# Second block: positions' tables are made in the first block; projections, outputs and feed-forward begin and end with one token tile ahead of the other

## The chip, the cores and the metric

The kernel runs on one core of a Trainium2 chip. The metric is the device time of one execution in microseconds (us); lower is better. Three executions of the kernel before took 2748.75, 2737.08 and 2747.66 us, median 2747.66.

Engines are named as the profile names them: PE (TensorE, matmuls), PEld (its weight loads), DVE (VectorE), ACT (ScalarE), POOL (GpSimd), SP (SyncE, which here issues every DMA).

## The reference, cut to what matters

Two transformer blocks of two layers each run one after the other over 256 tokens of width 1024, in float32. The change lies in the second block:

```python
def second_block(x, positions, ...):
    cos, sin = rope_tables(positions)
    for l in range(DEPTH):                                   # 2
        h = rms_norm(x, attn_pre_norm[l])
        mix = hybrid_mixer(h, cos, sin, w_in[l], ...)        # h @ w_in, three attentions, @ w_out
        x = x + rms_norm(mix, attn_post_norm[l])
        h = rms_norm(x, ffn_pre_norm[l])
        x = x + rms_norm(conv_ffn(h, w_up[l], conv_w[l], conv_b[l], w_down[l]), ffn_post_norm[l])
    return x

def rope_tables(positions):
    inv_freq = ROPE_THETA_2 ** (-2.0 * jnp.arange(half, dtype=jnp.float32) / ROPE_DIM)
    ang = positions.astype(jnp.float32)[..., None] * inv_freq
    return jnp.cos(ang)[:, :, None, :], jnp.sin(ang)[:, :, None, :]

def conv_ffn(h, w_up, conv_w, conv_b, w_down):               # w_up: 1024 x 5632, w_down: 2816 x 1024
    u = h @ w_up
    ...                                                      # causal convolution of 3 taps along the tokens
    a, b = jnp.split(c, 2, axis=-1)
    return (jax.nn.silu(a) * b) @ w_down
```

Each `rms_norm` needs a whole row of 1024, so a matmul that follows one can begin for a token only when the matmul before the norm has ended for that token in all of its columns.

## The kernel before, in words

The 256 tokens lie in two **token tiles** of 128 (tile 0 and tile 1). All large products are made from pairs: every float32 operand is split into a rounded `hi` part and the remainder `lo`, and `mm3` (L220 to L222) issues three matmuls for each pair of 128 x 128 weights. Weights come by DMA as `raw` blocks of 128 x 1024 (512 KB); ACT makes `hi` (L210, a cast) and DVE makes `lo` (L213, a subtraction) before PE can use them. The blocks of raw lie in a ring of a few buffers: SP issues the next one when the DVE subtraction has emptied a buffer.

`gemm_t` takes the activations as the stationary operand, so one matmul serves one token tile and 512 columns of output. It runs through blocks of weights (4 rows of 128 each) and does tile 0, then tile 1, for every block; the last `tail` blocks are held back and done for tile 0 first and then for tile 1. `gemm_f` (the up projections of the feed-forward) takes the weights as the stationary operand, so each of its matmuls covers 256 columns, the tokens of both tiles.

A layer of the second block is: `rms_hT` (norm, transposes, split), `attend` with six projections `proj(0)` to `proj(5)` (512 columns each, the last one 284) and the attention, `wide` (output projection, 2 column halves of 512, 8 rows of weights), `add_rms`, `rms_hT`, 22 up projections of 256 columns with the convolution between (L475, L477), `down` (2 column halves, 22 rows of weights), `add_rms`.

Between two products stands this chain for each tile, which I call a **seam**: L411 (ACT, squares of one column half), L412 (DVE), L274 and L275 (POOL, inverse root), L419 (DVE, adds into the stream X), L369 (ACT, squares of X), L274 and L275 again, L376 (ACT, tile 0) or L374 (DVE, tile 1) for the scaled row, 8 transposes on PE (L385 where `apart` is set: a PSUM tile holds 4 of them, all of one token tile; L395 otherwise: a PSUM tile holds both token tiles), and the split of the transposed tile: L313 (ACT) and L314 (DVE), in pieces of 128 or 256 columns. There are four seams that matter here: A, from the first block into layer 1; B, from `wide` into the feed-forward of layer 1; C, from `down` of layer 1 into layer 2; D, as B, in layer 2. At A the chain begins in the first block's own norm (L1012 to L1044).

The order of the instructions on each engine is not written out by hand: the framework's scheduler simulates the program and sets one queue per engine, and every engine takes its queue in that order. A matmul that stands behind a transpose in PE's queue waits when the transpose waits.

`positions` makes the sine and cosine tables of the second block: 11 small DVE operations on tiles of 128 x 16 and two ACT operations that need another function table (L346, L347). `consts2` casts two constant matrices. Both are called at the begin of the second block.

## Time and profile before

| what | value |
|---|---|
| three runs | 2748.75, 2737.08, 2747.66 us; median 2747.66 |
| the profiled execution | 2742.06 us, of which 2740.2 us is the span from its first to its last instruction |
| PE busy | 2640.3 us (96%) |
| DVE, ACT, POOL busy | 1955.6 us (71%), 1383.8 us (50%), 136.0 us (5%) |
| mean granted TensorE clock | 0.98 |
| first block, second block | about 0 to 2014 us, 2014 to 2740 us |

All terms in the text are differences against the profiled execution; the time to be predicted is a median of runs, which stands 5.6 us (0.2%) above that execution.

### The profile page before, as it was taken

What the parts mean: (1) busy time and instruction counts of PE and PEld (TensorE: products, weight loads), DVE (VectorE), ACT (ScalarE), POOL (GpSimd) and SP (SyncE); (2) the same over time, 40 slices, a digit from 0 to 9 for tenths busy, and PEclk for the clock granted to TensorE, in tenths of its full rate; (3) what the DMA queues carried; (4) which work ended last, traced back from release to release, by engine and by line L of the source; (5) the groups of instructions that cost most, each with busy time, mean ns of one, the idle gap of its engine ahead of it and who ended that gap; (6) DMA issues with size and microseconds to landing.
All of it is one profiled execution on the core that took longest, in us unless ns stands there. A gap on an engine that the chain in (4) does not pass through costs nothing.

```text
span 2740.2 us, 44882 instructions
## 1 busy us (share of the span) xinstructions
PE 2640.3 (96%) x17024; PEld 2260.7 (83%) x17024; DVE 1955.6 (71%) x3942; ACT 1383.8 (50%) x2524; POOL 136.0 (5%) x280
## 2 busy tenths in 40 slices
PE   7999999999999999999999999989999999999999
PEld 5877999977889888887797898879976699776897
DVE  4988977888866633345688997666666698556895
ACT  3555565545545422234745654544454566544663
POOL 0010011000001100002100100010010000000000
PEclk9999999999999999999999999989999999998999
DMA  7566556565535522222555433545554256542454
GB/s 255 185 229 205 170 171 217 173 205 177 178 116 193 185 85 93 93 96 91 155 170 202 156 128 116 169 154 193 186 186 156 89 185 195 173 149 80 167 192 155
DMA packets 127912, 443.29 MB, mean 162 GB/s; under 512 B 14888, under 2 KB 19112, under 8 KB 127696
## 3 DMA queue, kind: packets, MB, share of 16 engines
q1 hardware_dynamic: 127696, 440.43, 48.7%
q8 instruction: 134, 2.20, 0.3%
q14 instruction: 82, 0.67, 0.1%
HBM read 435.09 MB, written 5.28 MB: 161 GB/s over the span
## 4 chain that ended last, share of the span: by engine, by line
PE 87%; DVE 4%; DMA 3%; ACT 3%; issue 1%; POOL 1%; SPq 0%; DVEq 0%; POOLq 0%; ACTq 0%
PE g L221 20%; PE g L220 20%; PE g L222 20%; PE t L221 3%; PE t L222 3%; PE t L220 3%; DMA raw<-in_w_dram 2%; PE g L919 2%; PE t L1142 2%; PE t L1168 1%; PE t L1270 1%; PE t L1255 1%; PE t L1105 1%; DVE lo L213 1%; PE g L663 1%
## 5 line engine op out<-in xcount | busy, mean ns | idle before, releaser
L213 DVE TENSOR_TENSOR lo<-raw,hi 128x512 fp32r<-128x512 f32 (+2 forms) x1280 | 825.3, 684 | 350.4 <-issue 156.7
L210 ACT CAST hi<-raw 128x1024 fp32r<-128x1024 f32 (+2 forms) x644 | 671.9, 1045 | 723.9 <-PE g L221 252.3
L220 PE MATMUL g<-b,hi 128*128 128x256 f32 (+1 forms) x2912 | 831.1, 287 | 2.5 <-ACT hi L210 1.8
L221 PE MATMUL g<-b,hi 128*128 128x256 f32 (+1 forms) x2912 | 827.7, 286 | 2.7 <-DVE b L311 2.6
L222 PE MATMUL g<-b,lo 128*128 128x256 f32 (+1 forms) x2912 | 822.3, 287 | 1.6 <-DVE lo L213 1.6
L220 PEld LDWEIGHTS g<-b,hi 128*128 128x128 f32 x2912 | 548.2, 189 | 13.5 <-ACT b L310 2.4
L221 PEld LDWEIGHTS g<-b,hi 128*128 128x128 f32 x2912 | 548.6, 188 | 12.4 <-DVE b L311 4.3
L222 PEld LDWEIGHTS g<-b,lo 128*128 128x128 f32 x2912 | 541.5, 188 | 11.0 <-DVE lo L213 2.7
L1282 DVE SCALAR_TENSOR_TENSOR yc<-yc,vec,yc 128x256 f32<-128x256 f32 x720 | 345.7, 480 | 10.9
L221 PE MATMUL g<-lo,b 128*128 128x512 f32 (+2 forms) x712 | 271.8, 382 | 1.8 <-DVE lo L213 1.7
L220 PE MATMUL g<-hi,b 128*128 128x512 f32 (+2 forms) x712 | 253.5, 376 | 11.8 <-ACT hi L210 6.2
L222 PE MATMUL g<-hi,b 128*128 128x512 f32 (+2 forms) x712 | 264.2, 371 | 0.5 <-DVE b L314 0.4
L220 PEld LDWEIGHTS g<-hi,b 128*128 128x128 f32 x712 | 134.0, 191 | 38.6 <-ACT hi L210 7.0
L221 PEld LDWEIGHTS g<-lo,b 128*128 128x128 f32 x712 | 135.7, 191 | 30.5 <-DVE lo L213 6.3
L222 PEld LDWEIGHTS g<-hi,b 128*128 128x128 f32 x712 | 135.3, 190 | 22.2 <-DVE b L314 1.1
L220 PE MATMUL t<-b,hi 128*128 128x256 f32 (+1 forms) x336 | 111.9, 333 | 0.0
L221 PE MATMUL t<-b,hi 128*128 128x256 f32 (+1 forms) x336 | 111.9, 333 | 0.0
L222 PE MATMUL t<-b,lo 128*128 128x256 f32 (+1 forms) x336 | 111.7, 332 | 0.0
L919 PE MATMUL g<-raw,cs 128*32 128x512 f32 x384 | 84.4, 637 | 12.4 <-DMA raw<-in_w_dram 12.2
L477 DVE SCALAR_TENSOR_TENSOR s<-g,vec,s 128x255 f32<-128x255 f32 (+1 forms) x176 | 84.2, 478 | 6.0 <-ACT s L475 3.8
L221 PEld LDWEIGHTS t<-b,hi 128*128 128x128 f32 x336 | 63.2, 188 | 7.5
L220 PEld LDWEIGHTS t<-b,hi 128*128 128x128 f32 x336 | 63.1, 188 | 7.4
(421 smaller groups left out, 3924.1 us busy)
## 6 DMA issues: line engine op xcount, KB each, us to landing
raw<-in_w_dram SPq DMA_DIRECT2D x772, 512.0 KB
b<-in_row_dram SPq DMA_DIRECT2D x16, 512.0 KB
b<-in_ctx_dram SPq DMA_DIRECT2D x4, 512.0 KB
ends<-st SPq DMA_DIRECT2D x8, 256.0 KB
st<-ends SPq DMA_DIRECT2D x8, 256.0 KB
b<-in_x_dram SPq DMA_DIRECT2D x4, 512.0 KB
b<-ctx SPq DMA_DIRECT2D x4, 512.0 KB
raw<-in_w_dram SPq DMA_DIRECT2D x4, 426.0 KB
```

Source lines behind the costliest of these rows:

```text
L210: self.nc.scalar.copy(hi[:, :m], p)
L213: self.nc.vector.tensor_sub(lo[:, q], p[:, q], hi[:, q].bitcast(F32))
L220: t.matmul(ps, a[0], b[0], start=first, stop=False)
L221: t.matmul(ps, a[0], b[1], start=False, stop=False)
L222: t.matmul(ps, a[1], b[0], start=False, stop=last)
L477: nc.vector.scalar_tensor_tensor(c[:, m, j:], ps[:, m, :256 - j], cw[:, ft, 2 - j:3 - j], c[:, m, j:], op0=ALU.mult, op1=ALU.add)
L663: nc.tensor.matmul(ps[:, b], qk['nq', a * per + b][s, t * 128:t * 128 + 128], qk[kn, 0][s, :nk], start=False, stop=b == per - 1)
L919: nc.tensor.matmul(ps[32 * q:32 * q + 32], self.cs[:, h * 4 + q], raw[:, q % 2 * 512:q % 2 * 512 + 512], start=h == 0, stop=h == 1, tile_p ...
L1105: nc.tensor.matmul(p[:, h], kw[:, d, h * 128:h * 128 + 128], vg[:, h * 256:h * 256 + 256], start=True, stop=True)
L1142: nc.tensor.matmul(o, w, self.U[d][:, b * 256:b * 256 + n], start=d + i == 0, stop=d + i == 2)
L1168: nc.tensor.matmul(ps[:, a, h], G[h][b][:, a] if b < 3 else kT[:, h, ts], G[h][b][:, 2 + a], start=True, stop=True)
L1282: e.scalar_tensor_tensor(o, y[:, j:j + 256], w[:, j:j + 1], o, op0=ALU.mult, op1=ALU.add)
```

## The change

- `consts2` and `positions` are called in the first block, ahead of its last feed-forward, and their tiles go to the pool that lives through the whole program. `positions` loads the 128 x 8 table of frequencies by a DMA of its own.
- `attend` calls `proj(1, 2)` first, then `proj(5)`; `proj(1)` used to come later, behind the gates. With `ahead=2` both of its blocks are the tail, so tile 0 goes through all 8 rows of weights before tile 1. All its weights lie in the buffers of tag `zh` (those of the feed-forward's z tiles).
- `wide` calls the steps of its two column halves in turn, one at a time; it called one step of each half and then two of each.
- In the feed-forward `rms_hT` is called with `apart` set, and the first two up projections (f = 0) are made with the activations stationary, tile by tile: 48 matmuls of 256 columns for each tile, an ACT copy of 128 x 512 out of PSUM and 4 transposes back for each tile.
- `down` holds back 1 block in its first half and 3 in its second (1 and 2 before).
- A scratch area of the DMAs is set to 1024 bytes.

```diff
-                hi = self.tile(pool or self.slot(), [128, cols], F32R, tag or 'hi')
-                lo = self.tile(pool or self.W, [128, cols], F32R, tag or 'lo')
+                th, tl = tag if isinstance(tag, tuple) else (tag or 'hi', tag or 'lo')
+                hi = self.tile(pool or self.slot(), [128, cols], F32R, th)
+                lo = self.tile(pool or self.W, [128, cols], F32R, tl)
...
-    def positions(self, pos):
-        nc = self.nc
+    def positions(self, pos, freq):
+        nc = self.nc
+        fq = self.tile(self.S, [128, 8], F32, 'freq')
+        nc.sync.dma_start(fq, freq)
...
-        self.identb = self.tile(self.P, [128, 128], BF16, 'identb')
+        self.identb = self.tile(self.C, [128, 128], BF16, 'identb')
...
-        def proj(c):
+        def proj(c, ahead=0):
+
             n = 512 if c < 5 else 284
             pss = [self.tile(self.PG, [128, 512], F32, 'g')[:, :n] for _ in range(2)]
-            self.gemm_t(pss, xs, self.blocks(lambda h: src('in', c, h) if c < 5 else src('inr', 0, h), 8, n))
+            tiles = self.blocks(lambda h: src('in', c, h) if c < 5 else src('inr', 0, h), 8, n, ahead, (self.P, 'zh', 512))
+            self.gemm_t(pss, xs, tiles, tail=ahead or 1)
...
-            for n in (1, 2):
+            for _ in range(3):
                 for st in steps:
-                    for _ in range(n):
-                        next(st, None)
+                    next(st, None)
             return pss
         self.add_rms(X, wide, row[:, :D])
 
 
-        hT = self.rms_hT(X, v[:, V2['fn']:V2['fn'] + 8])
+        hT = self.rms_hT(X, v[:, V2['fn']:V2['fn'] + 8], True)
         cw = v[:, V2['cw']:].rearrange("p (f j) -> p f j", j=4)
         zh, zl = [], []
+
+        ws = [self.weights(src('up', e), 8, 256, *at) for e, at in enumerate(((), (self.P, 'zh', 512)))]
+        first = []
+        for t in range(2):
+            ts = slice(t * 128, t * 128 + 128)
+            ps = self.tile(self.PG, [128, 512], F32, 'g')
+            for e, w in enumerate(ws):
+                for k in range(8):
+                    self.mm3(ps[:, e * 256:e * 256 + 256], (hT[0][:, k, ts], hT[1][:, k, ts]), w[k], e + k == 0, e == 1 and k == 7)
+            y = self.tile(self.P, [128, 512], F32, 's2')
+            nc.scalar.copy(y, ps)
+            first = first or [self.tile(self.PT, [128, 2, 256], F32, 't') for _ in range(2)]
+            for e in range(2):
+                for m in range(2):
+                    col = e * 256 + m * 128
+                    nc.tensor.transpose(first[e][:, m, ts], y[:, col:col + 128], self.ident)
         for f in range(11):
             cc = []
             for half in range(2):
-                w = self.weights(src('up', 2 * f + half), 8, 256)
-                ps = self.tile(self.PG, [128, 2, 256], F32, 'g')
-                self.gemm_f([ps[:, m] for m in range(2)], w, lambda k: (hT[0][:, k], hT[1][:, k]))
+                if f == 0:
+                    ps = first[half]
+                else:
+                    w = self.weights(src('up', 2 * f + half), 8, 256)
+                    ps = self.tile(self.PG, [128, 2, 256], F32, 'g')
+                    self.gemm_f([ps[:, m] for m in range(2)], w, lambda k: (hT[0][:, k], hT[1][:, k]))
...
-            self.gemm_t(ps, zs, self.blocks(lambda h: src('down', c, h), 22, 512, 2 * c, (self.P, 'zh', 512)), tail=1 + c)
+            self.gemm_t(ps, zs, self.blocks(lambda h: src('down', c, h), 22, 512, 2 * c, (self.P, 'zh', 512)), tail=1 + 2 * c)
...
         nc = self.nc
+        proj(1, 2)
         proj(5)
...
         nc.vector.scalar_tensor_tensor(lf, z, 0.0, e, op0=ALU.min, op1=ALU.subtract)
-        proj(1)
...
                     else:
+                        K.consts2(I['cm'])
+                        n, m = AT2['freq']
+                        K.positions(I['pos'], I['cst2'][:, n:n + m])
                         K.pend = left(K.ffn(L, X))
```

Since the scheduler sets the queues, the program's own order is shown at three places. In the rows of the changed kernel, line numbers lie 1 to 3 higher: L211 is the cast L210, L221 to L223 are the three matmuls L220 to L222, L372, L379, L388 and L414 are L369, L376, L385 and L411.

**ACT at seam C**, from the first tile's last squares to the second tile's norm. Names: `ms_...77` and `ms_...94` belong to tile 0's sums, `b_1720` and `b_1721` are tiles 0 and 1 of X, `h<-raw` are weights of `proj(1)`, `hi<-raw` of 852 and 284 columns are weights of `proj(5)`. Before:

```order
L411 ACTIVATE b_4079_24086,ms_4077_24084<-g_24305 128x512
L369 ACTIVATE b_4158_24531,s_n_4162_24538<-b_1720_10158 128x1024
L411 ACTIVATE b_4080_24087,ms_4078_24085<-g_24306 128x512
L376 ACTIVATE b_4158_24531<-b_1720_10158,s_n_4164_24541 128x512 x2
L313 ACTIVATE b_4170_24559<-t_24560,vec_3468_20826 128x128
L313 ACTIVATE b_4170_24559<-t_24573,vec_3468_20826 128x128
L369 ACTIVATE b_4159_24532,s_n_4167_24551<-b_1721_10159 128x1024
```

The same place after the change:

```order
L414 ACTIVATE b_4096_24136,ms_4094_24134<-g_24355 128x512
L211 CAST h_4199_24672<-raw_24666 128x512
...
L372 ACTIVATE b_4175_24581,s_n_4179_24588<-b_1720_10158 128x1024
L211 CAST h_4209_24692<-raw_24686 128x512
L414 ACTIVATE b_4097_24137,ms_4095_24135<-g_24356 128x512
L211 CAST hi_24760<-raw_24758 128x852
L211 CAST h_4212_24698<-raw_24696 128x512
L379 ACTIVATE b_4175_24581<-b_1720_10158,s_n_4181_24591 128x512 x2
L211 CAST hi_24767<-raw_24765 128x284
L211 CAST h_4214_24702<-raw_24696 128x512
L372 ACTIVATE b_4176_24582,s_n_4184_24601<-b_1721_10159 128x1024
```

Where no cast stood, nine now stand inside the chain: seven of 128 x 512 (three of them in the line of "..."), one of 852 and one of 284 columns.

**PE at seam C**, changed kernel, from tile 0's transposes on (`b_4175` is tile 0, `b_4176` tile 1):

```order
L388 MATMUL t_24610<-cst_6_81,b_4175_24581 128x128 x4
L388 MATMUL t_24623<-cst_6_81,b_4175_24581 128x128 x4
L221 MATMUL g_24664<-h_4197_24668,b_4187_24609 128x512
L222 MATMUL g_24664<-h_4198_24669,b_4187_24609 128x512
L388 MATMUL t_24636<-cst_6_81,b_4176_24582 128x128 x4
L388 MATMUL t_24649<-cst_6_81,b_4176_24582 128x128 x4
L223 MATMUL g_24664<-h_4197_24668,b_4187_24609 128x512
```

Two matmuls of tile 0 stand between the two tiles' transposes; before, 8 matmuls of 284 columns stood there. At seam A these are 6 of 512 columns, and 6 of 284 before.

**PE at seam B**, changed kernel, the same place (`b_3859` is tile 0, `b_3860` tile 1):

```order
L388 MATMUL t_22432<-cst_6_81,b_3859_22403 128x128 x4
L388 MATMUL t_22445<-cst_6_81,b_3859_22403 128x128 x4
L221 MATMUL g_22518<-hi_22486,b_3871_22431 128x256
L222 MATMUL g_22518<-lo_22487,b_3871_22431 128x256
L223 MATMUL g_22518<-hi_22486,b_3871_22431 128x256
...
L388 MATMUL t_22458<-cst_6_81,b_3860_22404 128x128 x4
L388 MATMUL t_22471<-cst_6_81,b_3860_22404 128x128 x4
L223 MATMUL g_22518<-hi_22486,b_3871_22431 128x256
```

Eight matmuls of tile 0 (three shown) stand between the tiles' transposes, where none stood before; the other 88 of the first two up projections come behind tile 1's transposes. D is the same. Ahead of B, the last matmuls of `wide` stand as before: both kernels end it with 10 matmuls of tile 1 for one column half and 10 for the other. The last matmuls of `down` are 20 of tile 0 and then 20 of tile 1; they were 18 and 18.

## Rows read from the trace of the kernel before

**Rows 1.** The page: busy time and share of PE; the chain that ended last, by engine.

```profile
PE 2640.3 (96%) x17024; PEld 2260.7 (83%) x17024; DVE 1955.6 (71%) x3942; ACT 1383.8 (50%) x2524; POOL 136.0 (5%) x280
...
PE 87%; DVE 4%; DMA 3%; ACT 3%; issue 1%; POOL 1%; SPq 0%; DVEq 0%; POOLq 0%; ACTq 0%
```

**Rows 2.** Waits of PE, 2014 to 2740 us: total us, times, longest.

```profile
PE t L385 <- ACT b L376: 7.7, 2, 5.7
PE t L395 <- DVE b L374: 6.1, 2, 3.2
...
PE t L395 <- ACT b L376: 3.3, 2, 1.9
```

**Rows 3.** Seam A, timeline: start us, us, engine, line, operation [idle <-releaser].

```profile
2019.78 1.97 PE L385 MATMUL t<-cst,b 128*128 128x128 f32 x8 [5.69 <-ACT b L376]
2024.75 1.11 PE L385 MATMUL t<-cst,b 128*128 128x128 f32 x4
...
2024.61 1.28 ACT L347 ACT_TABLE_LOAD   x1
2025.91 0.22 ACT L347 ACTIVATE cs<-ang 128x16 f32<-128x16 f32 x1
...
2044.76 1.28 ACT L444 COPY proj<-g 128x512 f32<-128x512 f32 x2 [1.76 <-PE g L222]
...
2024.21 0.48 DVE L374 TENSOR_SCALAR b<-b,s_n 128x512 f32<-128x512 f32 x1
```

**Rows 4.** What a piece of work takes: casts, subtractions, splits, arrival of a raw block.

```profile
2163.67 3.73 ACT L210 CAST h<-raw 128x512 fp32r<-128x512 f32 x7
...
2164.32 4.30 DVE L213 TENSOR_TENSOR h<-raw,h 128x512 fp32r<-128x512 f32 x7 [0.55 <-ACT h L210]
...
2026.41 1.92 DVE L314 SCALAR_TENSOR_TENSOR b<-t,vec,b 128x128 fp32r<-128x128 f32 x6 [0.44 <-ACT b L313]
...
2356.24 3.50 SPq L190 DMA_DIRECT2D raw<-in_w_dram  x4
...
2360.13 1.14 ACT L210 CAST h<-raw 128x512 fp32r<-128x512 f32 x2 [2.75 <-DMA raw<-in_w_dram]
```

**Rows 5.** Seam C, timeline.

```profile
2366.58 0.39 PE L220 MATMUL g<-h,h 128*128 128x512 f32 x1
...
2370.43 0.39 PE L222 MATMUL g<-h,h 128*128 128x512 f32 x1
2372.80 1.27 PE L385 MATMUL t<-cst,b 128*128 128x128 f32 x8 [1.98 <-ACT b L376]
...
2377.24 1.91 PE L385 MATMUL t<-cst,b 128*128 128x128 f32 x8
...
2372.02 1.33 ACT L376 ACTIVATE b<-b,s_n 128x512 f32<-128x512 f32 x2 [0.42 <-POOL s_n L275]
...
2396.78 1.28 ACT L444 COPY proj<-g 128x512 f32<-128x512 f32 x2 [1.73 <-PE g L222]
...
2376.50 0.88 DVE L374 TENSOR_SCALAR b<-b,s_n 128x512 f32<-128x512 f32 x2
```

**Rows 6.** Seam B, timeline: the transposes of tile 1.

```profile
2185.80 1.97 PE L395 MATMUL t<-cst,b 128*128 128x128 f32 x8 [3.16 <-DVE b L374]
```

**Rows 7.** Windows: length; busy (instructions) of PE, PEld, DVE, ACT, POOL; granted clock; DMA share; GB/s.

```profile
2186.00:2192.00 6.00, 6.00 (x30) 5.94 (x30) 3.43 (x9) 3.15 (x8) 0.00 (x0) 0.54 0.01 3
2192.00:2200.00 8.00, 8.00 (x73) 8.00 (x72) 5.48 (x10) 4.09 (x5) 0.00 (x0) 1.00 0.42 131
2376.00:2380.00 4.00, 4.00 (x20) 3.94 (x21) 3.24 (x11) 2.36 (x9) 0.47 (x1) 0.59 0.00 0
2549.00:2555.00 6.00, 5.63 (x32) 5.57 (x33) 4.01 (x10) 3.15 (x8) 0.00 (x0) 0.64 0.01 3
...
0.00:40.00 40.00, 25.75 (x108) 8.12 (x108) 8.13 (x23) 8.70 (x14) 3.04 (x26) 0.91 0.87 290
40.00:2014.00 1974.00, 1927.85 (x12566) 1674.92 (x12565) 1431.18 (x2801) 984.93 (x1784) 116.64 (x219) 0.99 0.49 161
```

More of the change, by code (lines that the diff above doesn't have):

```diff
@@ L263, in blocks @@
             hs[-2:] = hs[:-3:-1]
-        own = hs[len(hs) - last:]
-        return [(4 * h, lambda h=h: self.weights(src(h), min(4, n - 4 * h), ncol, *(at if h in own else ()))) for h in hs]
+        own = dict(zip(hs[len(hs) - last:], at if at and isinstance(at[0], tuple) else (at,) * last))
+        return [(4 * h, lambda h=h: self.weights(src(h), min(4, n - 4 * h), ncol, *own.get(h, ()))) for h in hs]
     def small(self, fam, n=8):
@@ L356, in consts2 @@
         for t in range(2):
-            b = self.tile(self.P, [128, 512], BF16, f'cmb{t}')
+            b = self.tile(self.C, [128, 512], BF16, f'cmb{t}')
             nc.vector.tensor_copy(b, raw[:, t * 512:t * 512 + 512])
@@ L1763, in build @@
             K.c = lambda n: c2[:, AT2[n][0]:AT2[n][0] + AT2[n][1]]
-            K.consts2(I['cm'])
-            K.positions(I['pos'])
             for l in range(2):
```

4 lines of the change are left out of this document (2 added, 2 removed).

## The prediction, made before the changed kernel was run

> **What bounds the kernel now.** The page comes first: PE is busy for 2640.3 of 2740.2 us, and the chain that ended last runs through PE for 87% of the span [rows 1]. DVE (71%) and ACT (50%) matter only where PE waits for them. The changed kernel issues the same matmuls and 16 more transposes, so time can only come from PE's waits and from stretches at the lower clock. The next view is therefore the waits of PE in the second block. Three kinds belong to the seams: 7.7 us for L376 with tile-wise transposes (A 5.7, so C 2.0), 6.1 us for L374 (B 3.2, D 2.9), 3.3 us for L376 at B and D [rows 2]. That is 17.1 us, about 0.6% of the run, and most of it is a chain that the change keeps. The timeline of each seam tells what the wait is for, and the windows tell the clock: behind the waits it is granted 0.54 at B and 0.64 at D, near the lower of the two levels (1.2 and 2.4 GHz), and 1.00 right behind that [rows 7].
>
> **The change part by part.** What matters is when tile 1's transposes can start, since nearly all of PE's work stands behind them, and PE's queue keeps its order. I call that moment the restart.
>
> *`wide`:* the diff lets tile 0 end earlier, but the program's order shows the same last 20 matmuls of tile 1 in both kernels. The scheduler had already done it. Term: 0.
>
> *`down`:* tile 0 ends 20 instead of 18 matmuls ahead. A matmul of 512 columns takes 0.2265 us ((2370.43 − 2366.58) / 17 [rows 5]), so tile 0's chain starts 0.45 us earlier; this is inside the walk of seam C. At the program's end tile 1's chain is last in both kernels: 0.
>
> *Seam C.* PE ends at 2370.66 (the last matmul's start [rows 5] and one step); I count from there. Before, L376 starts at +1.36, L374 at +5.84, the restart is at +6.58 [rows 5]. Now nine weight casts and their subtractions stand inside this chain. A cast of 128x512 takes 0.53 us (3.73 / 7), a subtraction 0.61 us (4.30 / 7) [rows 4]; the 852-column cast I scale to 0.9 us. Walking both queues with these: tile 0's L369 starts at −0.95, since a subtraction stands ahead of L419; tile 1's L411 starts at +0.8 behind one cast; two casts (0.9 and 0.55) hold L376 until +2.95; tile 1's L369 starts at +5.15, L374 at +7.35, restart at about +8.1. So the restart is 1.5 us later. Ahead of it PE does 2 matmuls of 512 columns (0.45 us) where it did 8 of 284 (each 284/512 of 0.2265, 0.126; 1.0 us): another 0.55 us. Against that, from 2377.24 to the copy at 2396.78 [rows 5] PE took 19.5 us for 17.9 us of work at full clock (1.27 for transposes, 40 × 0.126, 48 × 0.2265, 0.7 for six small matmuls): 1.6 us went to waits and the lower clock, and a restart with more splits ready may save some. Between +0.45 (all of the 1.6 saved) and +2.05 (none) I take **+1.5**. Bounds: −1 if the casts find idle time and the restart does not move; +5 if all nine (3.73 + 0.9 + 0.3) lie in series.
>
> *Seam A.* The same with eight casts and subtractions of `proj(1)` and two of `proj(5)` in the norm's chain. `positions` leaves: 1.28 us of table load, 2 × 0.22 us on ACT [rows 3], about 2.7 us of small DVE work, and a reload of the gates' table. In the walk tile 0's L376 is 0.9 us later, tile 1's L1042 1.1 us later (behind three subtractions), its L369 2.3 us later (behind five casts), and L374 moves from 2024.21 [rows 3] to about 2027.5: 3.3 us. What `positions` gave back is in that; most of it stood behind the point where the chain is now held. Restart at 2028.0; behind it lie 1.27 + 42 × 0.2265 + 48 × 0.126 = 16.8 us. Before, 2024.75 to 2044.76 [rows 3] took 20.0 us for 18.1 us of work, of which 0.7 us (the small matmuls) now comes later and is not counted. With the same loss of 1.9 us the end is at 2046.7 against 2044.1: +2.6; with no loss +0.7. One more wait: the second 852-column block can be issued only when a subtraction at about 2026.8 has emptied its buffer, and a block arrives 3.9 us after its issue (2356.24 to 2360.13 [rows 4]). ACT stands at its cast then, ahead of the split of row 2: up to +0.9. I take **+2.5**; bounds −2.5 (restart unmoved, no loss) and +4.
>
> The Trainium skill, ScalarE: Activation LUTs, section What ACT_TABLE_LOAD costs, gives a table load about 1.28 us and a drain of about 1.38 us beside it. The trace has the 1.28 us, and the next operation 0.02 us behind it [rows 3], so no drain is seen. By the page A would get up to 1.4 us more back.
>
> *Where `positions` goes:* the scheduler puts it at the program's start, some 25 us in. There the DMA is the pace (0.87 busy, PE 25.75 of 40 us [rows 7]), which hides it: 0. Without that cover it costs about 5 us (two table loads of 1.28, 0.44 for the tables, about 2 for the small operations). The matrices' casts fall into the first block's feed-forward, 0.
>
> *Seams B and D.* PE now has eight matmuls of tile 0 ahead of tile 1's transposes, but tile 1's chain, which set the restart at 2185.80 [rows 6], is as long as before, and a few splits stand in it: 0.15 us later. Of the wait of 3.16 us [rows 6] only 8 × 0.11 us (8.00 / 73 [rows 7]) = 0.9 us is filled with work; the rest of the wait remains. The transposes back are 8 more, 1.27 us at full clock [rows 5]. That is +0.5 us at each. The splits are 16 pieces of 128 columns, each 0.32 us on DVE (1.92 / 6 [rows 4]), 5.1 us together, less than the 40 matmuls of tile 0 and the transposes need meanwhile: hidden; if not, 1 us. The clock pays: at B 30 matmuls and transposes took 6.0 us where 0.11 each would be 3.3, so 2.7 us lost; at D 5.63 against 3.5, 2.1 us lost [rows 7]. At C, where a few matmuls lie between the two tiles' transposes, the clock was back (0.59 in 2376 to 2380) within about 3 us of the first of them, sooner than at B. I take half as regained: B 0.5 − 1.3 = **−0.8**, D 0.5 − 1.0 = **−0.5**. Bounds: −2.2 and −1.6 (all regained), +1 each (none, and a split late).
>
> Sum: 1.5 + 2.5 − 0.8 − 0.5 = **+2.7 us**. On the profiled execution (2742.06) that is 2744.8, on the median (2747.66) 2750.4. The three runs spread over 11.7 us, so I do not trust either to the us, and predict the middle, **2748 us**.
>
> **The rivals.**
>
> 1. *The clock is not regained.* The few matmuls between the transposes are too thin, and the stretch behind the restart is as slow as now. For it: at B the matmuls run near the lower level although 8 transposes had run right ahead of them [rows 6, 7]. Against it: C. B and D are then +0.5 each, the sum +5.0: about 2750.
> The Trainium skill, TensorE: Matmul & The Clock Gate, section Part 4: PE-mode transpose, says that transposes do not count as PE activity the way matmuls do. By that rule the transposes that now come earlier would earn no clock, which is this case; the trace does not separate it from the plain effect of the wait.
>
> 2. *It hides what it is built to hide.* The casts find idle slots of ACT and DVE (C −1, A −2.5) and the clock comes back at once (B −2.2, D −1.6): −7.3 us, some 2738. For it: ACT is half idle [rows 1]. Against it: in the seam ACT is the chain.
>
> 3. *The casts lie in the chain one after the other, and a block of weights comes late* (the other side). Place: ACT's queue at C, where the 852-column cast stands ahead of tile 0's L376. It decides once that block arrives later than about +1.6 us, which is when my walk has it arrive, 3.9 us behind a subtraction that ends at −2.25: then L376, both tiles and PE wait for a DMA. Price: up to the +5 of C and +4 of A, with +1 for B and D: +10 us, some 2756.
>
> 4. *The scheduler's new order of the first block matters.* About 7% of PE's rows there stand elsewhere. PE is idle for 46 of 1974 us in it [rows 7]; were a third of that added or taken away, which is my guess of how far an order can go, it would be 15 us either way.
>
> **How the numbers follow.** Forecast 0.50 (its own range 2742 to 2754), rival 1 0.17, rival 2 0.13, rival 3 0.12, rival 4 0.08, half on each side. A measurement of this kernel can tell about 0.5%, 13.7 us, from no change: below 2734 or above 2761. Forecast and rival 1 lie inside. Rival 2 gets past 2734 one time in four, rival 4's good half most times: 0.06. Rival 3 gets past 2761 one time in three, rival 4's bad half most times: 0.08. The range leaves out half of rival 4 on each side and the tails of rivals 2 and 3: 2736 to 2760.
>
> **What would show it.** In the profile after: at C L376 some 1.6 us and tile 1's transposes some 1.5 us later against the end of `down`, with casts of `h` between L411 and L376; at A tile 1's transposes about 3 us later against the first block's last matmul, and no table load ahead of the splits; at B and D a wait of 1 to 2 us ahead of tile 1's transposes with eight matmuls ahead of it, and fewer slow matmuls behind. I am wrong where tile 1's transposes come earlier at A or C, where ACT waits for a raw block ahead of L376, or where the first block's length differs by more than 5 us.

## The result, and the profile after

| kernel | median of the runs | profiled execution | span | PE busy |
|---|---|---|---|---|
| before | 2747.4 us (4 runs, 2737.1 to 2748.8) | 2742.06 us | 2740.2 us | 2640.3 us |
| after | 2783.3 us (4 runs, 2780.5 to 2786.4) | 2781.47 us | 2779.6 us | 2670.7 us |

The ratio is 1.0134, 95% interval 1.0115 to 1.0154: slower by about 37 us. The prediction was 2748 us with a range up to 2760, so it was wrong. Line numbers of after are 1 higher than before up to L314 (L313 before), 3 higher up to L422, 23 higher behind the feed-forward.

The page of after, against [rows 1]:

```profile
PE 2670.7 (96%) x17040; PEld 2289.2 (82%) x17040; DVE 1954.8 (70%) x3958; ACT 1391.8 (50%) x2556; POOL 136.6 (5%) x280
...
PE 22%; ACT 1%; DVE 1%; DMA 1%; issue 0%; POOL 0%; DVEq 0%; POOLq 0%; ACTq 0%; SPq 0%
```

The first line already says that the prediction looked in the wrong place. Of the 39 us between the spans PE is idle for 9 and busy for 30, with 16 instructions more, and 16 transposes are worth 2.5 us at the 1.27 us that 8 of them take at full clock [rows 5]. (The second line is of no use: the chain could be followed back for a quarter of the span only.) The waits of PE from seam A on, against [rows 2], account for little of it:

```profile
PE t L388 <- ACT b L379: 17.3, 4, 6.4
PE g L221 <- ACT b L314: 7.4, 4, 3.3
...
PE g L221 <- ACT hi L211: 1.3, 2, 1.1
```

The 17.1 us of the three seam waits before are 17.3 us now, all ahead of tile 0's transposes (L388, which stands where L385 and L395 stood), and new are 7.4 us in which the early matmuls of tile 0 wait for its splits (L314). So busy PE has to be read next, and since the granted clock is 1.00 nearly everywhere, by how many matmuls it gets done. Windows of PE over 25 us of the feed-forward in layer 1 and in layer 2; first before, then after (length, busy, number of matmuls, clock, DMA share, GB/s):

```profile
2220.00:2245.00 25.00, 25.00 (x223) 1.00 0.60 197
2583.00:2608.00 25.00, 25.00 (x223) 1.00 0.59 194
```

```profile
2254.00:2279.00 25.00, 25.00 (x214) 1.00 0.56 190
2616.00:2641.00 25.00, 25.00 (x214) 1.00 0.56 187
```

PE is never idle in these windows, the clock is the full one in all four, the work is the same (256 columns, `gemm_f`), and after does 4% fewer matmuls. The timeline shows the step, before:

```profile
2250.17 0.28 PE L221 MATMUL g<-b,hi 128*128 128x256 f32 x1
2250.28 0.28 PE L222 MATMUL g<-b,lo 128*128 128x256 f32 x1
2250.40 0.28 PE L220 MATMUL g<-b,hi 128*128 128x256 f32 x1
```

and after:

```profile
2250.23 0.28 PE L223 MATMUL g<-b,lo 128*128 128x256 f32 x1
2250.35 0.28 PE L221 MATMUL g<-b,hi 128*128 128x256 f32 x1
2250.47 0.28 PE L222 MATMUL g<-b,hi 128*128 128x256 f32 x1
```

The duration of one (0.28) is the same; the distance from start to start is 0.113 before and 0.118 to 0.12 after. I took it from the starts of all neighbouring matmuls of equal width at full clock: with 256 columns 115.08 ns before (9250 pairs) and 118.44 after (9273); with 512 columns 231.9 and 232.8 (3800 pairs). 9270 × 3.36 ns is 31.1 us and 3810 × 0.84 is 3.2 us: 34 of the 39 us between the spans. It is so in the first block too, which the change hardly touches: its last matmul starts at 2042.0 instead of 2013.7. (Not all of that is the step: in e3 below, which has the instructions of before and their step, it starts at 2025.5.) What the change says it does is not what it costs.

### The profile page after: what moved, and what is told of

The parts are those of the page before. It is cut to its first block, busy times and chain, and to the rows that moved or that the text cites. A ratio compares the mean times of both kernels' runs of the same rounds, so it can differ in the third digit from the quotient of the medians.

```text
span 2779.6 us, 44965 instructions
## 1 busy us (share of the span) xinstructions
PE 2670.7 (96%) x17040; PEld 2289.2 (82%) x17040; DVE 1954.8 (70%) x3958; ACT 1391.8 (50%) x2556; POOL 136.6 (5%) x280
## 5 line engine op out<-in xcount | busy, mean ns | idle before, releaser
L214 DVE TENSOR_TENSOR lo<-raw,hi 128x512 fp32r<-128x512 f32 x1256 | 808.8, 683 | 387.3 <-issue 151.2
L211 ACT CAST hi<-raw 128x1024 fp32r<-128x1024 f32 (+1 forms) x632 | 658.7, 1044 | 703.9 <-PE g L222 273.4
L221 PE MATMUL g<-b,hi 128*128 128x256 f32 (+2 forms) x2848 | 820.0, 290 | 1.4 <-ACT hi L211 0.7
L222 PE MATMUL g<-b,hi 128*128 128x256 f32 (+2 forms) x2848 | 817.4, 288 | 2.8 <-DVE b L312 2.8
L223 PE MATMUL g<-b,lo 128*128 128x256 f32 (+2 forms) x2848 | 814.3, 290 | 1.3 <-DVE lo L214 1.1
L221 PEld LDWEIGHTS g<-b,hi 128*128 128x128 f32 (+1 forms) x2848 | 534.9, 188 | 12.6 <-ACT b L311 2.7
L222 PEld LDWEIGHTS g<-b,hi 128*128 128x128 f32 (+1 forms) x2848 | 535.1, 188 | 12.3 <-DVE b L312 4.5
L223 PEld LDWEIGHTS g<-b,lo 128*128 128x128 f32 (+1 forms) x2848 | 529.9, 188 | 11.2 <-DVE lo L214 2.8
L222 PE MATMUL g<-lo,b 128*128 128x512 f32 (+2 forms) x712 | 268.7, 379 | 3.0 <-DVE lo L214 2.9
L223 PE MATMUL g<-hi,b 128*128 128x512 f32 (+2 forms) x712 | 261.6, 368 | 0.0
L221 PE MATMUL g<-hi,b 128*128 128x512 f32 (+2 forms) x712 | 251.6, 372 | 7.5 <-ACT h L541 3.6
L221 PEld LDWEIGHTS g<-hi,b 128*128 128x128 f32 x712 | 133.8, 190 | 34.9 <-ACT h L541 4.4
L222 PEld LDWEIGHTS g<-lo,b 128*128 128x128 f32 x712 | 135.7, 191 | 31.9 <-DVE lo L214 8.8
L223 PEld LDWEIGHTS g<-hi,b 128*128 128x128 f32 x712 | 135.7, 191 | 21.2 <-DVE b L315 0.3
L221 PE MATMUL t<-b,hi 128*128 128x256 f32 (+1 forms) x336 | 112.8, 336 | 0.0
L223 PE MATMUL t<-b,lo 128*128 128x256 f32 (+1 forms) x336 | 112.7, 336 | 0.0
L222 PE MATMUL t<-b,hi 128*128 128x256 f32 (+1 forms) x336 | 112.6, 335 | 0.0
L500 DVE SCALAR_TENSOR_TENSOR s<-g,vec,s 128x255 f32<-128x255 f32 (+1 forms) x160 | 71.7, 475 | 1.0 <-ACT s L498 0.4
L222 PEld LDWEIGHTS t<-b,hi 128*128 128x128 f32 x336 | 63.3, 188 | 7.3
L221 PEld LDWEIGHTS t<-b,hi 128*128 128x128 f32 x336 | 63.3, 188 | 7.2
```

The costliest lines, as they stand in the source:

```text
L211: self.nc.scalar.copy(hi[:, :m], p)
L214: self.nc.vector.tensor_sub(lo[:, q], p[:, q], hi[:, q].bitcast(F32))
L221: t.matmul(ps, a[0], b[0], start=first, stop=False)
L222: t.matmul(ps, a[0], b[1], start=False, stop=False)
L223: t.matmul(ps, a[1], b[0], start=False, stop=last)
L500: nc.vector.scalar_tensor_tensor(c[:, m, j:], ps[:, m, :256 - j], cw[:, ft, 2 - j:3 - j], c[:, m, j:], op0=ALU.mult, op1=ALU.add)
```

## The experiments

**What differs and isn't in the instructions.** `positions` takes a new tile of 32 bytes per partition (`freq`), and the three tiles of `consts2` go to another pool. Everything allocated behind them lies elsewhere in SBUF, the on-chip memory that PE reads from. The addresses can be read from the compiled programs. For the matmuls of 256 columns in `gemm_f` the streamed operand is `b16` (the transposed activations, two buffers), the stationary one is a piece of `hi` or `lo`. I call the start of the streamed one minus the start of the stationary one, in bytes of a partition, the **distance**. Inside the tiles the pieces lie a multiple of 256 bytes apart, so all matmuls on a pair of buffers have one distance modulo 256.

All runs; the middle columns are the distance modulo 256 of these streams and the matmuls in 25 us of the feed-forward, layer 1 and layer 2:

| run | instructions of | distance | x in 25 us | median us | ratio to before |
|---|---|---|---|---|---|
| before | before | 192 | 223, 223 | 2742 to 2747 | |
| after | after | 224 | 214, 214 | 2783.3 | 1.0115 to 1.0154 |
| e1_pad | after | 0 | 211, 211 | 2783.1 | 1.0118 to 1.0171 |
| e2_shift32 | before | 224 | 213, 214 | 2773.8 | 1.0086 to 1.0128 |
| e3_scratch | before | 192 | 223, 223 | 2745.5 | 0.9986 to 1.0014 |
| e4_all64 | after | 0 | 210, 211 | 2775.0 | 1.0100 to 1.0143 |
| e5_phase64 | after | 64 | 215, 215 | 2770.5 | 1.0086 to 1.0116 |
| e6_both32 | after | 64 | 215, 215 | 2778.3 | 1.0107 to 1.0144 |
| e7_before_best | before | 64 and 192 | 214, 223 | 2744.4 | 0.9993 to 1.0018 |
| e8_best | after | 192 and 64 | 223, 214 | 2749.1 | 1.0014 to 1.0036 |
| f1_phase192 | after | 192 | 223, 223 | 2750.0 | 0.9999 to 1.0035 |
| f2_shift128 | before | 64 | 214, 214 | 2759.3 | 1.0026 to 1.0061 |
| f3_after_256 | after | 192 | 214, 214 | 2740.4 | 0.9962 to 0.9991 |
| f4_before_256 | before | 192 | 215, 214 | 2734.7 | 0.9916 to 0.9964 |
| g1_noffn | part of after | 192 | 223, 223 | 2735.4 | 0.9957 to 0.9983 |
| g2_noproj | part of after | 192 | 223, 223 | 2734.6 | 0.9936 to 0.9980 |
| g3_neither | part of after | 192 | 223, 215 | 2733.2 | 0.9928 to 0.9970 |
| g4_before_again | before | 192 | 215, 223 | 2732.1 (one) | |
| h1_dist128 | part of after | 128 | 213, 213 | 2762.6 | 1.0047 to 1.0090 |
| h2_dist160 | part of after | 160 | 215, 211 | 2757.6 | 1.0030 to 1.0057 |

**e1 to e4: is it the address, and on which grid?** The edits, in this order:

```
+ fq = self.tile(self.S, [128, 16], F32, 'freq')[:, :8]     # e1, in after: 64 bytes for 32
+ pf = self.tile(self.S, [128, 16], F32, 'pf')[:, :2]       # e2, in before: 32 bytes more
+ bacc.Bacc(..., dynamic_dma_scratch_size=1024)             # e3, in before
+ pad = -cells % (64 // size)                               # e4, in after: tile() rounds sizes up
```

> The changed kernel with one edit: the frequencies' tile, 32 bytes per partition, takes 64 bytes, so that every tile allocated behind it starts 32 bytes higher; the instructions and their order are the same. Theory A (start addresses): in the changed kernel the rows that PE streams begin 32 bytes past a multiple of 64, where before they began on one, and a matmul of 256 columns takes 118.3 instead of 113.3 ns. Then this kernel has 223 matmuls in 25 us in the feed-forward of the second block (the changed kernel has 214) and takes 2738 to 2752 us. Rival B (the smaller scratch memory of the DMAs) and rival C (the new order of instructions on PE, ACT and DVE): nothing changes, 2779 to 2787 us.

> The kernel before with one edit: a small tile (two positions per partition) takes 64 bytes instead of 32, so that everything allocated behind it moves up by 32 bytes; nothing else. Theory A: the time of the changed kernel, 2775 to 2790 us, with 214 matmuls in 25 us in the feed-forward. Rivals B and C: 2737 to 2750 us, as before.

> The kernel before with one edit: the scratch memory of the DMAs is 1024 bytes, as in the changed kernel, which moves every tile down by 15360 bytes, a multiple of 64. Theory A: 2737 to 2750 us, as before. Rival B (the scratch memory costs the time): 2775 to 2790 us. Rival C: as before.

> The changed kernel with every tile's size rounded up to a multiple of 64 bytes, so that all start on one; in the kernel before, and in the changed kernel with the one tile padded, 47 weight tiles and the tiles of the feed-forward of the second block still start 32 bytes past one. Theory A, if it holds for the stationary side too: some 940 matmuls of 256 columns at 4 ns and up to 1300 of 512 columns at 2 ns, 3 to 7 us below the kernel with the one tile padded, about 2735 to 2745 us. If only the streamed side counts: as that kernel within 3 us. Rivals B and C: 2779 to 2787 us.

e2 and e3 settle two things. 32 bytes more in a tile of before, with every instruction the same, cost 29 us (2773.8 against 2744.8), most of what the change costs; the scratch memory costs nothing. So the address counts, and rivals B and C can't have the main part. But e1 and e4, on which theory A bet, stayed at 2783 and 2775: starting on a multiple of 64 is not the rule. In e1 the step was 119.8 ns, worse than in after. What orders the steps of the kernels so far is the distance modulo 128: 96 at 118.3 to 118.4 ns (after, e2), 0 at 119.8 (e1, e4), and 64 in the only fast ones (before, e3).

**e5 to e8: the distance modulo 128?** The edits: in e5 the tile of after takes 128 bytes; e6 is e5 with a scratch memory of 1056 bytes; e7 (before) and e8 (after) round sizes up to 128 and shift the streamed activations inside their buffers:

```
- t = self.tile(self.A, [128, 2, 8, 256], F32R, 'b16')
+ t = self.tile(self.A, [128, 4128], F32R, 'b16')[:, 16:4112].rearrange("p (a k n) -> p a k n", a=2, k=8)
```

> The changed kernel with the frequencies' tile taking 128 bytes instead of 32 and nothing else: what lies behind it starts 96 bytes higher. Theory A2, formed from the runs so far: what counts is where the streamed operand starts against the stationary one, modulo 128 bytes. For 256 columns a distance of 64 gives 113.3 ns a matmul (kernel before), 32 or 96 gives 118.4 (changed kernel, kernel before moved by 32), 0 gives 119.8 (one tile padded to 64, all tiles rounded to 64). Here the distance is 64 again with the instructions of the changed kernel: 223 matmuls in 25 us in the feed-forward, 2739 to 2752 us. Rival C (the new order of instructions): no change, 2774 to 2787 us.

> As the kernel with the tile of 128 bytes, and the scratch memory of the DMAs 32 bytes larger, so that streamed and stationary operands both move up by 32 bytes: streamed at 96 modulo 128, where they lie in the changed kernel, stationary at 32, distance 64. Theory A2 (the distance counts): 223 matmuls in 25 us, 2739 to 2752 us. Rival D (the place of the streamed operand itself counts, and 64 modulo 128 is the good one): 214 in 25 us, 2774 to 2787 us.

> The kernel before, same instructions, with tiles laid out for the distances: sizes rounded up to 128 bytes, so that all matmuls of 512 columns have a distance of 0 (227 to 228 ns in the runs so far, against 233 at other distances), and the activations that are streamed with 256 columns shifted by 64. Theory A2: some 910 first-block matmuls of 512 columns gain 6 ns, some 1100 whose stationary operand lay at 32 or 96 gain 5, some 900 of 256 columns whose weights lay at 96 gain 4: 14 us, so 2727 to 2735 us. Rival D: as before, 2737 to 2750 us.

> The changed kernel, same instructions, with the same layout of tiles. Theory A2: 2727 to 2738 us, 40 to 55 us below the changed kernel; against the kernel before in that layout it shows what the order of work alone is worth, which the prediction put at +2.7 us. Rival C: over 2760 us, since the order would cost on any layout.

e5 and e6 refuted this form of the theory (215 in 25 us), and e5 refuted rival D as well: it has the streamed operand at 64 modulo 128, where before has it. e7 and e8 gave the answer without being built for it. Rounding had made their two `b16` buffers 128 bytes out of step with each other, and the feed-forward of layer 1 uses one, that of layer 2 the other. Windows of e7:

```profile
2227.00:2252.00 25.00, 25.00 (x214) 1.00 0.59 187
2583.00:2608.00 25.00, 25.00 (x223) 1.00 0.59 191
```

and of e8:

```profile
2226.00:2251.00 25.00, 25.00 (x223) 1.00 0.63 203
2585.00:2610.00 25.00, 25.00 (x214) 1.00 0.59 191
```

The slow layer is the one whose buffer has a distance of 64, the fast one has 192. Modulo 256 the fast kernels (before, e3) have 192 and e5 and e6 have 64.

**f1 to f4: the distance modulo 256.** f1 is after with 256 bytes for `freq`, f2 is before with 128 bytes more; f3 (after) and f4 (before) round all sizes outside the small pools up to 256, so that the matmuls of 512 columns get a distance of 0 where both operands allow it, with the activations at 192 in both buffers (`[:, 48:4144]` in the edit above).

> The changed kernel with the frequencies' tile taking 256 bytes instead of 32, nothing else. Theory A3, from the steps of all ten profiles so far: the distance from the stationary to the streamed operand counts modulo 256 bytes. With 256 columns a distance of 192 gives 113.3 ns (kernel before), 64 gives 118 (tile of 128 bytes), 224 gives 118.4 (changed kernel), 0 gives 119.8. Here the distance is 192 with the instructions of the changed kernel: 223 matmuls in 25 us in the feed-forward of the second block and 2738 to 2752 us. Rival C (the order of instructions sets the mode of each stream): stays at 2766 to 2785 us.

> The kernel before with the small tile of positions 128 bytes larger, so that the distance is 64 modulo 256 and still 64 modulo 128. Theory A3: 214 to 216 matmuls in 25 us and 2764 to 2775 us, as the changed kernel had at that distance. If the distance counts modulo 128 alone, and the order of instructions did the rest: 2737 to 2750 us.

> The changed kernel, same instructions, sizes of tiles rounded up to 256 bytes so that matmuls of 512 columns have a distance of 0 (227 ns in the profiles so far, 233 at most other distances), and activations that are streamed with 256 columns a distance of 192 in both of their buffers. Theory A3: 2722 to 2735 us, below both kernels. Rival C: 2745 to 2785 us.

> The kernel before, same instructions, in the same layout of tiles. Theory A3: 2720 to 2732 us: 937 matmuls of 256 columns gain 4 to 5 ns and some 2000 of 512 columns 6 ns, 16 us together. Against it the changed kernel in this layout shows what the order of work is worth with the steps of the matmuls equal; the prediction put that at +2.7 us.

f1 decides: the instructions of after, 224 unused bytes more, and 33 us are gone (2783.3 to 2750.0). Its windows:

```profile
2237.00:2262.00 25.00, 25.00 (x223) 1.00 0.60 196
2598.00:2623.00 25.00, 25.00 (x223) 1.00 0.59 194
```

f2 went the other way by 15 us, less than expected. Its step of 256 columns is as slow as in e5 (117.7 ns over the whole program), but not its step of 512 (232.0 ns where after and e5 have 232.8), which is 3 us of the miss; the rest I can't place. f3 and f4 came out 5 and 3 us above the expected ranges. Their matmuls of 512 columns do what was expected (at a distance of 0, 2225 pairs at 226.7 ns, 99% of them below 228), but the feed-forward of the second block ran at 214 although the distance is 192. Windows of f3:

```profile
2218.00:2243.00 25.00, 25.00 (x214) 1.00 0.57 190
2577.00:2602.00 25.00, 25.00 (x214) 1.00 0.58 191
```

At 192 a stream has two steps, 113.3 and 117.8 ns, which I call its modes, and it can hold one of them for tens of us, the longest for some 120; over the first ten profiles 67% of the pairs were in the fast one, against 1 to 19% at 0, 32, 64, 96 and 224.

**g1 to g4: what the order of work itself costs.** In the layout of f3: g1 has the feed-forward of before, g2 has `proj(1)` back behind the gates, g3 both; g4 is f4 once more.

```
- hT = self.rms_hT(X, v[:, V2['fn']:V2['fn'] + 8], True)    # g1, g3; and first, ws and their loop go
+ hT = self.rms_hT(X, v[:, V2['fn']:V2['fn'] + 8])
...
- proj(1, 2)                                                # g2, g3
  proj(5)
...
+ proj(1)
```

> The changed kernel in the layout rounded to 256 bytes, with the feed-forward of the second block as before (no split by token tile, no transposes back). Measured from the last matmul of the stage ahead to the start of the 240th matmul behind it (the 248th where 8 transposes back are added): in that layout the kernel before takes 36.2 us at seam B and 36.1 at D, the changed one 37.7 and 37.1. Theory E (the feed-forward part costs there, since casts of its first weights stand ahead of tile 0's norm): B and D come back to 36.2 and 36.1 within 0.4 us, A and C stay at 62.5 and 57.4; 2 to 3 us less in all, which the time itself can hardly show. Rival F (the wide part, which is still in, costs there): B and D stay at 37.7 and 37.1.

> The changed kernel in the layout rounded to 256 bytes, with the projection of the second column block back at its old place behind the gates. Same measure: the kernel before takes 60.2 us at seam A and 55.9 at C, the changed one 62.5 and 57.4. Theory E: without the casts of that projection in the chain C comes back to 55.9 and A falls below 60.2 by what the tables' work took there, to 58 to 60; B and D stay at 37.7 and 37.1. Rival F (the down part, the moved tables or the longer chain at the end of the first block cost there): A and C stay at 62.5 and 57.4.

> The changed kernel in the layout rounded to 256 bytes, without both parts: of the change only the tables' place, the two edits of how weights are held back, and the scratch memory are left. Theory E: seams A 58 to 60, B 36.2, C 55.9, D 36.1; the time within 5 us of the kernel before in that layout (2734.7), so 2728 to 2738, the best of all. Rival F: as the changed kernel in that layout, 2735 to 2745.

> The kernel before in the layout rounded to 256 bytes once more, unchanged. At a distance of 192 its feed-forward of the second block ran at 117.8 ns a matmul, where the kernel before ran at 113.3 at the same distance. If each execution draws its mode, some stretches that were slow are fast now; if the program sets it, the same stretches are slow again, within a few per cent of their matmuls.

The measure, from the start of the last matmul of the stage ahead: to the 240th matmul at A and C, to the 112th at B and D, or the 120th where 8 transposes back are added (the transposes and f = 0). The expectations name the 240th there too. By that g1 has 34.0 and 34.7 and g2 36.5 and 36.2 (at the 248th), all below what was expected, because the mode of the feed-forward, which differs between these runs, tells in it:

| us | A, 240 | B, 112 or 120 | C, 240 | D, 112 or 120 |
|---|---|---|---|---|
| before | 60.0 | 20.7 | 55.3 | 20.2 |
| f4, g4 (before) | 60.2, 60.1 | 21.1, 19.9 | 55.9, 55.7 | 21.0, 20.0 |
| f3, f1 (after) | 62.5, 62.9 | 22.7, 23.8 | 57.4, 57.7 | 22.0, 21.7 |
| g1 (no feed-forward part) | 66.0 | 19.5 | 57.4 | 20.2 |
| g2 (no early projection) | 59.9 | 21.9 | 54.8 | 21.7 |
| g3 (neither) | 60.4 | 20.8 | 55.2 | 21.2 |

Theory E holds at C, B and D, seam by seam: the early projection costs 2.1 us at C (57.5 against 55.4), the feed-forward part 2.4 at B (22.8 against 20.4) and 1.3 at D (21.8 against 20.5), and each goes with its part, which rules out rival F there. Two of its numbers missed. At A g2 and g3 are at 60, not below, so that the tables' work leaving the seam gave back nothing that can be seen. And g1 has 66.0 at A: its clock was lower there (0.85 and 0.94 over 2015 to 2045 and 2045 to 2075, where f3 has 0.91 and 1.00 in the corresponding windows), which is one execution. The times of g1 to g3 lie within 2.2 us of each other and of f4; they can't rank the four. All of them beat both kernels; g3 has the lowest median, 2733.2 us, 0.3 to 0.7% below before.

g4 shows that the program alone does not set the mode. Windows of f4:

```profile
2217.00:2242.00 25.00, 25.00 (x215) 1.00 0.57 178
2576.00:2601.00 25.00, 25.00 (x214) 1.00 0.55 179
```

and of the same kernel once more:

```profile
2214.00:2239.00 25.00, 25.00 (x215) 1.00 0.59 188
2575.00:2600.00 25.00, 25.00 (x223) 1.00 0.61 194
```

Layer 2 was slow in the one and fast in the other; most stretches of the first block have about the same share of fast pairs in both. The two executions were on different chips, so that either the execution or the chip may draw it. The chip alone does not: f1, on that of f4, ran fast in both layers, and g3, on that of g4, slow in layer 2. A whole feed-forward of some 1000 matmuls in the slow mode costs 4.5 us.

**h1 and h2: the two distances not yet seen.** g3 with `[:, 32:4128]` and `[:, 40:4136]`.

> The kernel of the last runs without the feed-forward part and the early projection, in the layout rounded to 256 bytes, with the activations that are streamed with 256 columns at a distance of 128 instead of 192. No profile so far has that distance. Bounds from the others: if it were always at the good step of 113.3 ns (192 has it in some stretches and 117.8 in others), 223 matmuls in 25 us in every feed-forward and 2715 to 2728 us; if it is as 0 (119.8) or 224 (118.4), 209 to 214 in 25 us and 2755 to 2775 us.

> The same with a distance of 160, the other one that no profile so far has. Same bounds: 2715 to 2728 us if always at 113.3 ns, 2755 to 2775 us if at 118 to 120, and 2728 to 2742 us if it has two modes as 192.

Both are slow, 118.7 and 118.3 ns on the mean. So of eight distances 192 alone has the good step in most of its pairs: 60% over all 20 profiles, against at most 19% at any other.

## Why the prediction was wrong

**The step that failed.** It is the conclusion from the first view: "The changed kernel issues the same matmuls and 16 more transposes, so time can only come from PE's waits and from stretches at the lower clock." The same matmuls of 256 columns took 3% longer each, 118.44 ns for 115.08. Shown by f1 (the same instructions, 33 us less), e2 (the instructions of before, 29 us more) and within one execution by e7 and e8. The diff had it: a tile of 32 bytes in a pool that lies ahead of `b16`. The price was not in the trace of before as a row, but a hint was: there too some 256-column streams of the first block ran at 118 ns and others at 113, at equal clock, and I read one step per width from one place. With the distance of before the changed kernel took 2750.0 us (f1), inside the range; that is partly luck, since the terms for B and D had the wrong sign and the first block's 5.9 us below were not in the sum.

**Rival 4 (the first block's length)** is what the reader would have seen first, since the block grew by 28 us, and its sign for being wrong ("differs by more than 5 us") came true. Its mechanism, the new order, has a small part of that, at one place. ACT of before, in the gates of the first block's second layer:

```profile
1360.04 1.08 ACT L1073 ACTIVATE ch<-t 128x512 f32<-128x512 f32 x2
1361.01 1.15 ACT L1074 ACTIVATE ch<-ch 128x512 f32<-128x512 f32 x2
1362.18 1.28 ACT L1075 ACT_TABLE_LOAD   x1
1363.48 1.15 ACT L1075 ACTIVATE ch<-ch 128x512 f32<-128x512 f32 x2
```

and of after:

```profile
1376.83 0.60 ACT L1096 ACTIVATE ch<-t 128x512 f32<-128x512 f32 x1
1377.46 0.63 ACT L1097 ACTIVATE ch<-ch 128x512 f32<-128x512 f32 x1
1378.00 0.58 ACT L1096 ACTIVATE ch<-t 128x512 f32<-128x512 f32 x1
1378.60 1.28 ACT L1098 ACT_TABLE_LOAD   x1
1379.89 0.63 ACT L1098 ACTIVATE ch<-ch 128x512 f32<-128x512 f32 x1
1380.54 1.28 ACT L1097 ACT_TABLE_LOAD   x1
1381.83 0.64 ACT L1097 ACTIVATE ch<-ch 128x512 f32<-128x512 f32 x1
1382.49 1.28 ACT L1098 ACT_TABLE_LOAD   x1
1383.78 0.63 ACT L1098 ACTIVATE ch<-ch 128x512 f32<-128x512 f32 x1
```

The scheduler used to do both token tiles' absolute values, then both exponentials, then both logarithms. Now one tile's logarithm stands ahead of the other's exponential, and ACT loads three tables instead of one, 2.6 us more in a chain for which PE waits behind (`PE t L1128 <- DVE ch L1112`, 2.3 us, a wait that before doesn't have). From 1356.3 to 1379.5 before and from 1370.6 to 1399.7 after PE does nearly the same 120 matmuls: 23.2 and 29.1 us, 5.9 more. In all 13 profiles with instructions of after PE waits 1.9 to 2.4 us there, and the 20 matmuls around the wait take 7.8 to 8.1 us; in the seven with those of before it waits at most 1.1 us, and they take 3.3 to 4.5. g3 has it without the early projection and the feed-forward part, so one of the other edits brings it, and not the scratch memory alone, since e3 has the old order; that it is the place of `positions` and `consts2` is argued, not shown. The Trainium skill, ScalarE: Activation LUTs, section Rules for kernel authors, says to group functions by table set and finish one set before the next; the trace agrees, at 1.28 us a load.

**Seams A and C (+2.5 and +1.5): right.** Measured +2.5 at A (f3 and f1 against before, f4 and g4) and +2.1 at C, at the 240th matmul. How much of it is given back later stays open: at the 429th f3 stands 1.3 and 0.1 us behind f4, f1 2.8 and 3.4 behind before. After's transposes at C, against [rows 5]:

```profile
2415.31 1.27 PE L388 MATMUL t<-cst,b 128*128 128x128 f32 x8 [2.95 <-ACT b L379]
...
2419.89 1.91 PE L388 MATMUL t<-cst,b 128*128 128x128 f32 x8
...
2414.54 1.33 ACT L379 ACTIVATE b<-b,s_n 128x512 f32<-128x512 f32 x2
```

Counted from the last matmul's start (2411.97) tile 1's stand at +7.92 where they stood at +6.81: 1.1 later, predicted 1.5, with the casts of `h` between the chain's steps on ACT as described. L379 starts without waiting for a block of weights, so rival 3 did not act at its place; nor did rival 2, since no seam became shorter. At A tile 1's come 15.5 us behind the last matmul, 4.5 later than before and not 3.3 (the scaled row itself, L377, is 4.2 later). That the time at A is right all the same is two errors that cancel: some 2 us of this are made good behind the restart, where the prediction had 0.7.

**Seams B and D (−0.8 and −0.5): wrong in sign, +2.4 and +1.3.** The failed step is "tile 1's chain [...] is as long as before, and a few splits stand in it: 0.15 us later". In after tile 1's transposes stand 10.15 us behind the last matmul's start (2214.18), where they stood 6.23 behind it (2185.80 [rows 6] and 2179.57): 3.9 later.

```profile
2219.22 1.97 PE L388 MATMUL t<-cst,b 128*128 128x128 f32 x8 [4.65 <-ACT b L379]
...
2224.33 1.84 PE L388 MATMUL t<-cst,b 128*128 128x128 f32 x8
```

In the nine profiles with the feed-forward part they stand 8.1 to 10.2 us behind it at B and 7.8 to 9.2 at D, in the eleven without it 6.2 at B and 6.2 to 6.8 at D. ACT of after at B:

```profile
2212.17 1.14 ACT L211 CAST h<-raw 128x512 fp32r<-128x512 f32 x2 [2.26 <-DMA raw<-in_w_dram]
2213.22 0.59 ACT L414 ACTIVATE b<-g 128x512 f32<-128x512 f32 x1
...
2213.80 1.03 ACT L211 CAST hi<-raw 128x1024 fp32r<-128x1024 f32 x1
...
2218.45 1.34 ACT L379 ACTIVATE b<-b,s_n 128x512 f32<-128x512 f32 x2 [0.42 <-POOL s_n L276]
```

and of before:

```profile
2173.07 1.05 ACT L210 CAST hi<-raw 128x1024 fp32r<-128x1024 f32 x1 [0.79 <-DMA raw<-in_w_dram]
...
2175.34 0.60 ACT L411 ACTIVATE b<-g 128x512 f32<-128x512 f32 x1 [0.63 <-PE g L222]
...
2180.59 1.33 ACT L376 ACTIVATE b<-b,s_n 128x512 f32<-128x512 f32 x2
```

The casts are of the feed-forward's own first weights (in the program's order their tiles carry numbers behind those of the norm). At the two of 512 columns ACT stands 2.26 us for a block that comes late by DMA, and tile 0's last squares (L414) stand behind. Before, those squares start 4.23 us ahead of the last matmul's start (2179.57), after only 0.96 ahead (2214.18): 3.3 us, and L379 is as late, 4.27 behind it instead of 1.02. This is rival 3's mechanism, a block of weights that comes late ahead of a chain, at seams where the prediction did not place it, and ACT waiting for a raw block ahead of that norm was one of its signs of being wrong. At D the casts stand in the same place, but in after the last two waits for blocks ahead of these squares are 1.13 and 0.26 us, which goes with the smaller cost there. Such casts are not new: before too has three of these weights' casts ahead of the squares, and waits 0.79 us at the last. New is that the second block of the second up projection stands ahead as well, and a cast of 1024 columns for f = 1 between tile 0's last squares and tile 1's. That the scheduler wants them earlier because the first up projections now begin with tile 0 alone is argued, not shown.

**The clock at B and D: right in direction, smaller than thought.** After's windows behind tile 1's transposes, against [rows 7]:

```profile
2224.00:2230.00 6.00, 6.00 (x44) 6.00 (x45) 4.17 (x14) 3.24 (x10) 0.00 (x0) 0.84 0.01 3
```

```profile
2584.00:2590.00 6.00, 6.00 (x39) 6.00 (x38) 3.88 (x13) 3.22 (x10) 0.00 (x0) 0.69 0.02 4
```

The granted clock is 0.84 and 0.69 where it was 0.54 and 0.64, and 44 and 39 matmuls and transposes fit where 30 and 32 did: at 0.11 us each about 1.5 and 0.8 us, against 1.3 and 1.0 predicted. One execution of each tells little here, since the clock behind a seam differs from run to run. Over the 6 us from tile 1's first transpose the granted clock is 0.70 at B and 0.71 at D on the mean of the nine profiles with the feed-forward part (0.62 to 0.86), 0.61 and 0.58 on that of the eleven without it (0.50 to 0.77), and 5 and 7 more matmuls and transposes start in it: some 0.6 and 0.8 us. So rival 1, that nothing is regained, doesn't hold, but less than the predicted half is, and the late chain outweighs it.

**`positions` at the program's start (0)** was right about the start itself: PE starts 109 matmuls in the first 40 us, 108 before. If it is this edit that changed the order in the gates, its cost came 1350 us later. **`wide` and `down` (0)**: nothing speaks against it; g3, which has both without the two costly parts, has each of the four seams at most 0.2 us outside what before, f4 and g4 have there.

**The sum.** Of the 39 us between the profiled spans the matmuls' steps make 34, as worked out above. The seams (2.5 + 2.1 + 2.4 + 1.3 = 8.3) and the place in the first block (5.9) make 14 more; the direct comparison, at equal distances, gives less: f1 is 5.5 us above before (its interval is −0.3 to +9.6), e8 4.7 above e7, and f3 5.7 above f4 (2734.6 to 2745.6 against 2722.6 to 2738.6). Why 14 local us are some 5 at the end stays open; draws of the mode are of that size, and in the first block f3 ends 0.5 us ahead of f4 although it has the three table loads.

## What to carry to other kernels

- When a change adds, drops or moves a tile, compare where the operands of the costly streams lie before and after, and not only the order of instructions. Padding costs nothing to try, and it separates a change's idea from its side effect: without f1 the 33 us would have been blamed on the order.
- When a busy engine gets slower at the same clock, count instructions in a window of equal length. Busy share and mean duration both stay the same.
- Work that is started earlier brings its loads and casts forward too; on an engine that keeps its queue's order, look at which chain they now stand ahead of.

## What the runs showed of the hardware that was not expected

- The step of a float32 matmul stream whose weights change with every matmul depends on where the streamed operand starts against the stationary one, modulo 256 bytes. With 256 columns, mean over the pairs of the first ten profiles at that distance (128 and 160: of h1 and h2): 0: 119.8 ns; 32: 116.8 (few); 64: 117.3; 96: 118.9; 128: 118.7; 160: 118.3; 192: 114.9 (115.1 over all 20); 224: 118.4. With 512 columns 0 is the good one (226.7 in f3 and f4, 228.0 over the first ten), 64 lies between (230.5), 128 is at 231.7 and the others at 233 to 234.
- That it is the distance and not the start of the streamed operand alone, e5 to e8 cannot show: in the streams that they compare the stationary operand starts at 128 modulo 256, except in e6. Short streams of the first block separate the two. In before, e3 and f1 some 420 pairs each have the streamed start of the fast streams (64) against a stationary start of 224, distance 96, and take 119.3 ns. In e8 152 pairs have the streamed start of its slow streams (192) against a stationary start of 0, distance 192, and take 113.5. Another 124 pairs of e8 fit less well: 64 against 0, distance 64, at 115.3.
- The Trainium skill, TensorE: Matmul & The Clock Gate, section Step-by-step: what each phase is for, says that the streamed operand and the weights are read through two independent ports, so that loading the next weights takes nothing from the running matmul. By that the step should not depend on the distance; here it goes from 113.3 to 119.8 ns, and the measurement decides. What in the hardware does it no run here shows.
- At a distance of 192 a stream can hold one of two steps, 113.3 or 117.8 ns, for tens of us, and f4 and g4 show one program with different steps in the same stretch. With the lower clock in some stretches it may be a part of why the runs of before spread over 12 to 24 us; no run separates the two.
